# Layer 1's output projection: y's hi and lo in one tile, buffers of their own for the last weights, gate sums as fp32r products

## The chip, the cores and the metric

The kernel runs on one core of a Trainium2 chip. The metric is the device time of one execution in microseconds (us). A profiled execution also has a span, from its first to its last instruction, and all positions below are us from the start of that span.

## The reference

Two trunk layers work on a latent stream x (256 tokens, 2048 wide) and a context stream (256 tokens). Cut to what matters here:

```python
shift, scale, gate = jnp.split(silu_c @ w_mod[l] + b_mod[l], 3, axis=-1)
h = rmsnorm(x, g_pre[l]) * (1.0 + scale[:, None]) + shift[:, None]
proj = h @ w_in[l]
y = mixer_branches(proj, latent_attn, ...)        # 256 x 2048: gMLP, window attention, Fourier parts
y = rmsnorm(y @ w_out[l], g_post[l])
x_new = x + gate[:, None] * y
```

The change is in the last two lines for the last layer: `y @ w_out[1]`, and the gate, which is a row of 2048 numbers made from `silu_c @ w_mod[1]`, `b_mod[1]` and `g_post[1]`.

## The kernel before, in words

**Products in parts.** A number in fp32 is kept as a pair hi + lo of two fp32r tiles: ACT casts it to hi (`A.copy`), DVE subtracts hi from it to get lo. A product of two such pairs is three TensorE products into one sum in PSUM, hi·hi, hi·lo and lo·hi: `mm3`, L405 to L407. In layer 1 the main products of the input projection use `mm2` (L521, L522) instead, on tiles `hh[k]` that hold hi in the columns 0 to 255 and lo in 256 to 511 (for the latents); `hl[k]` holds the same for the context, and is last read by the units k and v.

**Weights.** `Stream` brings all weights in tiles of 128x1024. `load` (L362) issues the DMA of one tile from SP into `raw`, which has three buffers. `emitting` (L367) casts it on ACT into `whi` (L383) and subtracts on DVE into `wlo` (L385); both have four buffers. Tiles named in `self.place` get hi and lo in other buffers: `TAIL` does that for the last four tiles of all (mraw; macc and ws/bsb; yo8 to yo15). `fetch` emits the tiles up to three ahead of the one that is asked for.

**Order.** PE's order is as written. The order of ACT, DVE, SP and POOL is laid out when the program is built, by a planner that goes by its own estimates of times, takes what is ready, and prefers what is written earlier. On the chip each engine then works through its list in that order and stands before an instruction whose operand or buffer isn't there.

**Layer 1's output projection** is `finish` (L961). The 2048 output columns are four chunks c of 512. Each chunk has eight weight tiles, two k (blocks of 128 rows of `w_out`) in each, and two token blocks t: `products` (L983) makes 3 matmuls of 512 columns for one (k, t), with y's parts `hh[k]`, `hl[k]` as the stationary operand. They are made at the end of `layer` (L921 to L925), hi into a fresh `hh[i]`, lo into a fresh `hl[i]`. In the last chunk t=1 runs eight k behind t=0 (`BACK`), so that all its eight tiles stay in use to the end. `evac` (L988) squares the sums on ACT (L990) and multiplies them by the gate on DVE (L992); `close` ends each token block with the norm, the residual and the output DMAs.

**The gate.** `mod_gate1` (L233) forms for each chunk `g1[c]`, a 128x512 tile, in the buffers ctrh, ctrl, nstrh and nstrl: sixteen DVE steps (L242, L244) with weights that SP loads into `mraw` (two buffers). Its column sums, spread over all partitions, come from one product with a tile of ones, in fp32 (L257). `gate1` also loads two rows into ws and bsb (L255) and finishes the gate with two DVE instructions (L258, L259). `GATES` says behind which k of which chunk `gate1(c)` is written. `pace` steps `mod_gate1` along with the weight tiles.

**Later work** is kept in `Later`: generators that say how long they want to wait before their next step; `tick` moves the clock by the time of the products just written. `turn` (L965) runs so in this stage and makes the residual: 32 transposes on PE, eight copies on ACT. `w2k` is a pool of seven tiles for passing work, `join` one of two.

Of the kernel before, what the change touches and what calls it, by code (L numbers as in the profile page):

```python
# [13 lines left out]
P = 128  # L14
# [52 lines left out]
def trunk_kernel(ctx: ExitStack, tc: tile.TileContext, xT, xhalf, cT, wss, wsl, wmod, win, wout0, wout1, const, vec, rows,  # L67
# [9 lines left out]
    def sb(shape, dt, tag, bufs=1):  # L77
        cnt[0] += 1
        return pool.tile(shape, dt, tag=tag, bufs=bufs, name=f"{tag}_{cnt[0]}")
# [8 lines left out]
    def ms_ps(name="ms"):  # L88
        cnt[0] += 1
        return psum.tile([P, 512], F32, tag="ms", bufs=2, name=f"ps_{name}_{cnt[0]}")  # L90
# [160 lines left out]
    def gate1(c):  # L251

        r = [sb([P, 512], F32, tag) for tag in ("ws", "bsb")]
        for i in range(2):
            DMA.dma_start(r[i], rows[None, i, c * 512:(c + 1) * 512].to_broadcast([P, 512]))  # L255
        ps = ms_ps("gate")
        PE.matmul(ps, ones, g1[c], start=True, stop=True)  # L257
        V.tensor_tensor(out=g1[c], in0=r[0], in1=ps, op=ALU.add)  # L258
        V.tensor_tensor(out=g1[c], in0=g1[c], in1=r[1], op=ALU.mult)  # L259

    def mod_rest():
        yield from mod_four(0, range(8, 12))
# [16 lines left out]
    MIDDLE = 3  # L279
    LOWC = 60  # L280
    YT = 3.0
    GATES = {4: 0}, {0: 1}, {0: 2, 14: 3}, {}
    YH = 2.0
    NX, LATE = 4, 6
    YX, YR, YC, YE = 1.0, 0.8, 1.5, 5.0
# [11 lines left out]
    class Later:  # L297
# [19 lines left out]
        def flush(self):  # L317
# [4 lines left out]

    HELD = 3
    NHI, NLO, NRAW = 4, 4, 3
    TAIL = [(("mraw", 2), ("mraw", 2)), (("macc", 1), ("ws bsb", 1)),
            (("yo8 yo9", 1), ("yo10 yo11", 1)), (("yo12 yo13", 1), ("yo14 yo15", 1))]
    AU2 = [(("hh12 hl12", 1), ("hh13 hl13", 1)), (("yo4 yo5", 1), ("yo6 yo7", 1))]
    BACK = 8


    class Stream:
        AHEAD = 3

        def __init__(self):
            self.src, self.out, self.pos, self.stop = [], [], 0, 0
            self.raws = []
            self.place, self.behind = {}, {}
            for l in range(2):
                def half(name, i, h):
                    return win[l, UIDX[name][i], h]  # L340
                for i in range(2):
                    a = [half("av", 2 * i, 0), half("au01", i, 0), half("av", 2 * i, 1),
                         half("av", 2 * i + 1, 0), half("au01", i, 1), half("av", 2 * i + 1, 1)]
                    if l == 0:
                        a.insert(3 - i, half("au2", 0, i))
                        self.place[len(self.src) + 3 - i] = AU2[i]
                    self.src += a
                for i, u in enumerate(UNITS):
                    if u[0] not in ("av", "au01") + ("au2",) * (l == 0):
                        self.src += [win[l, i, 0], win[l, i, 1]]  # L350
                if l == 0:
                    self.src += [wout0[j, i] for j in range(KT) for i in range(2)]
                else:
                    self.src += [wout1[c, i] for c in range(4) for i in range(8)]
                if l == 0:
                    n = len(self.src) - 2 * HELD
                    self.place[n] = (("mraw", 2), ("mraw", 2))
                    self.place[n + 1] = (("macc", 1), ("mg", 1))
            for i, tags in enumerate(TAIL):
                self.place[len(self.src) - len(TAIL) + i] = tags  # L360

        def load(self):  # L362
            r = sb([P, 1024], F32, "raw", NRAW)
            DMA.dma_start(r, self.src[len(self.raws)])
            self.raws.append(r)

        def emitting(self, cut=1024):  # L367

            if len(self.raws) == len(self.out):
                self.load()  # L370
            n = len(self.out)
            r = self.raws[n]
            tags = self.place.get(n, (("whi", NHI), ("wlo", NLO)))
            hi, lo = ([sb([P, 1024 // len(t[0].split())], F32R, tag, t[1]) for tag in t[0].split()] for t in tags)
            self.out.append((hi, lo))
            cut = min(cut, 1024 // max(len(hi), len(lo)))
            for i in range(0, 1024, cut):
                c = slice(i, i + cut)
                ph, pl = part((hi, lo), c)
                with ExitStack() as after:  # L380
                    for i in self.behind.get(n, ()):
                        after.enter_context(tc.issue_after(i.ins))
                    A.copy(ph, r[:, c])  # L383
                yield
                self.last = V.tensor_tensor(out=pl, in0=r[:, c], in1=ph.bitcast(F32), op=ALU.subtract)  # L385
                yield

        def emit(self):
# [164 lines left out]
    def layer(l):  # L553
# [366 lines left out]

        src = [ysl(k) for k in range(KT)]  # L921
        for i, k in enumerate(ORDER):
            new_h(i)
            A.copy(hh[i][:, 0:n], src[k])
            V.tensor_tensor(out=hl[i][:, 0:n], in0=src[k], in1=hh[i][:, 0:n].bitcast(F32), op=ALU.subtract)  # L925


    def o_evac(j, ps, o, acc, streams, first):
# [32 lines left out]
    def finish():  # L961

        x1 = {}

        def turn():  # L965

            for j, tag in enumerate(("vv", "mg", "mgl", "kt0 kt1")):
                tag = tag.split()
                tl = [sb([P, 2 // len(tag), 512], F32, t) for t in tag]
                for t in range(2):  # L970
                    x1[j, t] = tl[0][:, t] if len(tl) == 1 else tl[t][:, 0]
                    ps = ms_ps("x1")
                    for i in range(4):
                        PE.transpose(ps[:, i * P:(i + 1) * P], yo[4 * j + i][:, t * P:(t + 1) * P], ident)
                    A.copy(x1[j, t], ps)
                    yield YT

        later.add(turn(), YT)
        state["phase"] = "out1"
        sums = sb([P, 2, 4], F32, "sums")  # L980
        gy = {}
        tot = sb([P, 2], F32, "tot")
        def products(c, k, t, ps):  # L983
            ts = slice(t * P, (t + 1) * P)
            mm3(ps, (hh[k][:, ts], hl[k][:, ts]), part(w[k // 2], slice((k % 2) * 512, (k % 2 + 1) * 512)),
                k == 0, k == KT - 1)

        def evac(c, t, ps):  # L988
            gy[c, t] = sb([P, 512], F32, f"yo{2 * c + t}")
            A.activation(w2k([P, 512]), ps, AF.Square, accum_out=sums[:, t, c:c + 1])  # L990
            if c < 3:
                V.tensor_tensor(out=gy[c, t], in0=ps, in1=g1[c], op=ALU.mult)  # L992
            if c == 2:
                V.tensor_reduce(out=tot[:, t:t + 1], in_=sums[:, t, 0:3], axis=mybir.AxisListType.X, op=ALU.add)
                V.tensor_scalar(out=tot[:, t:t + 1], in0=tot[:, t:t + 1], scalar1=1.0 / D, scalar2=EPS,  # L995
                                op0=ALU.mult, op1=ALU.add)

        def close(t, ps):
            ms, r = (sb([P, 1], F32, t, 2) for t in ("rs_a", "rs_b"))
            V.tensor_scalar(out=ms, in0=sums[:, t, 3:4], scalar1=1.0 / D, scalar2=tot[:, t:t + 1], op0=ALU.mult,  # L1000
                            op1=ALU.add)
            G.tensor_tensor(out=r, in0=ms, in1=mhalf[:, 0:1], op=ALU.pow)
            V.tensor_tensor(out=gy[3, t], in0=ps, in1=g1[3], op=ALU.mult)
            for c, i, n in ((0, 0, 256), (0, 256, 256), (1, 0, 512), (3, 0, 512), (2, 0, 512)):
                sl = slice(i, i + n)
                o = gy[c, t][:, sl]
                if c == 3:
                    A.activation(o, o, AF.Copy, scale=r)
                    G.tensor_tensor(out=o, in0=o, in1=x1[c, t], op=ALU.add)
                else:  # L1010
                    V.scalar_tensor_tensor(out=o, in0=o, scalar=r, in1=x1[c, t][:, sl], op0=ALU.mult, op1=ALU.add)
                DMA.dma_start(out[t * P:(t + 1) * P, c * 512 + i:c * 512 + i + n], o)

        for c in range(4):
            pss = [mm_ps("y") for _ in range(2)]
            back = BACK if c == 3 else 0
            w = []
            for k in range(KT + back):
                if k < KT:
                    if k % 2 == 0:  # L1020
                        w.append(W.next())
                    products(c, k, 0, pss[0])
                if k == KT - 1:
                    evac(c, 0, pss[0])
                    if c == 3:
                        close(0, pss[0])
                if k >= back:
                    products(c, k - back, 1, pss[1])
                later.tick(PASS * 1024)
                if k in GATES[c]:  # L1030
                    gate1(GATES[c][k])
            evac(c, 1, pss[1])
        close(1, pss[1])

# [225 lines left out]
```

## Time and profile before

| | us |
|---|---|
| median of 3 runs | 1153.36 (1153.26 to 1154.21) |
| profiled execution | 1155.53 |
| its span | 1153.70 |
| PE busy | 1137.0, 99% of the span |
| DVE busy | 883.0, 77% |
| ACT busy | 521.6, 45% |
| first ps_y product (output projection of layer 1) starts | 1046.56 |
| last ps_y product ends | 1145.40 |

In the profile, PE is TensorE's matmuls, DVE VectorE, ACT ScalarE, POOL GpSimd, SP the engine that issues the DMAs. A matmul's length in the profile holds its way through the array, and lengths of successive matmuls overlap, so the cost of one is read from the starts of its neighbours. The granted clock is a share of TensorE's full speed; over the whole span it is 0.997. A group of instructions is named by line, engine, operation, and out<-in by the program's names of tiles without their numbers. A wait for several semaphores is put down to the one that came last by the profile, which need not be the true one. The span is read by stretches, and then one engine at a time in order of time.

### The profile page before, as it was taken

How to read it: one execution, taken by the hardware profiler on the slowest of the kernel's cores; microseconds unless marked ns; L12 is line 12 of the kernel's file. 1: busy time of each engine (PE TensorE's matmuls, PEld its weight loads, DVE VectorE, ACT ScalarE, POOL GpSimd, SP SyncE). 2: the span in 40 equal slices, each digit the busy share in tenths (PEclk: the TensorE clock that was granted, in tenths of full speed). 3: DMA queues.
4: the chain of work that ended last, by engine and by line, in shares of the span. 5: the costliest groups of instructions: out<-in, count | busy, mean ns of one | idle time of the engine just before them, and what ended most of it. 6: DMA issues, size and time to landing. Idle time of an engine off the chain costs nothing.

```text
span 1153.7 us, 17000 instructions
## 1 busy us (share of the span) xinstructions
PE 1137.0 (99%) x6391; PEld 935.2 (81%) x6391; DVE 883.0 (77%) x1496; ACT 521.6 (45%) x956; POOL 32.4 (3%) x39
## 2 busy tenths in 40 slices
PE   8999999999999999999999999999999999999996
PEld 3566688888898888888888888888888988888875
DVE  1545479999988887888999993396988688868774
ACT  5322343322224667632532323366665279846441
POOL 0000000000000000000000000200500000000001
PEclk9999999999999999999999999999999999999998
DMA  9999756566665343355566654365956666556972
GB/s 353 403 369 340 253 183 182 168 220 213 202 185 198 108 124 126 116 188 180 164 203 217 218 183 146 110 193 182 219 164 202 204 215 195 171 164 221 297 233 107
DMA packets 72227, 234.30 MB, mean 203 GB/s; under 512 B 8400, under 2 KB 11600, under 8 KB 72144
## 3 DMA queue, kind: packets, MB, share of 16 engines
q1 hardware_dynamic: 69840, 231.11, 61.4%
q0 software_dynamic: 2304, 2.10, 1.2%
q8 instruction: 50, 0.82, 0.3%
q14 instruction: 33, 0.27, 0.1%
HBM read 231.08 MB, written 2.10 MB: 202 GB/s over the span
## 4 chain that ended last, share of the span: by engine, by line
PE 85%; DMA 8%; DVE 4%; issue 2%; ACT 1%; SPq 0%; POOL 0%; DVEq 0%; ACTq 0%; POOLq 0%
PE ps_t L405 15%; PE ps_t L407 15%; PE ps_t L406 15%; PE ps_t L521 10%; PE ps_t L522 5%; DMA mraw<-in_wmod_dram 3%; PE ps_mod L169 2%; PE ps_av L405 2%; PE ps_av L406 2%; PE ps_av L407 2%; PE ps_tp L849 2%; DVE wlo L385 1%; PE ps_v L406 1%; PE ps_v L407 1%; PE ps_v L405 1%
## 5 line engine op out<-in xcount | busy, mean ns | idle before, releaser
L383 ACT CAST whi<-raw 128x1024 fp32r<-128x1024 f32 (+1 forms) x218 | 226.6, 1043 | 342.4 <-PE ps_t L406 222.7
L385 DVE TENSOR_TENSOR wlo<-raw,whi 128x1024 fp32r<-128x1024 f32 (+1 forms) x218 | 263.6, 1213 | 74.9 <-ACT whi L383 73.1
L405 PE MATMUL ps_t<-hh,whi 128*128 128x512 f32 (+1 forms) x768 | 294.2, 383 | 1.0 <-ACT yo L709 1.0
L407 PE MATMUL ps_t<-hh,wlo 128*128 128x512 f32 (+1 forms) x768 | 292.6, 381 | 0.0
L406 PE MATMUL ps_t<-hl,whi 128*128 128x512 f32 (+1 forms) x768 | 292.5, 381 | 0.0
L206 DVE SCALAR_TENSOR_TENSOR macc<-mraw,cs,macc 128x512 f32<-128x512 f32 x360 | 249.6, 748 | 17.8 <-DMA mraw<-in_wmod_dram 17.7
L521 PE MATMUL ps_t<-hh,whi 128*128 128x512 f32 x512 | 185.2, 400 | 0.0
L405 PEld LDWEIGHTS ps_t<-hh,whi 128*128 128x128 f32 x768 | 144.4, 188 | 29.1 <-issue 1.5
L407 PEld LDWEIGHTS ps_t<-hh,wlo 128*128 128x128 f32 x768 | 144.4, 188 | 27.9
L406 PEld LDWEIGHTS ps_t<-hl,whi 128*128 128x128 f32 x768 | 144.5, 188 | 26.0 <-issue 0.2
L522 PE MATMUL ps_t<-hh,wlo 128*128 128x256 f32 x512 | 143.1, 280 | 0.0
L521 PEld LDWEIGHTS ps_t<-hh,whi 128*128 128x128 f32 x512 | 96.2, 188 | 21.2 <-issue 0.2
L522 PEld LDWEIGHTS ps_t<-hh,wlo 128*128 128x128 f32 x512 | 96.5, 189 | 0.2 <-issue 0.2
L487 ACT ACTIVATE hh<-w2k,sh 128x256 fp32r<-128x256 f32 x48 | 21.9, 503 | 82.3 <-DVE w2k L483 82.3
L405 PE MATMUL ps_y<-whi,hh 128*128 128x512 f32 x112 | 46.4, 415 | 0.6 <-ACT whi L383 0.6
L406 PE MATMUL ps_y<-wlo,hh 128*128 128x512 f32 x112 | 44.2, 394 | 1.2 <-DVE tot L995 1.2
L407 PE MATMUL ps_y<-whi,hl 128*128 128x512 f32 x112 | 44.2, 395 | 0.0
L405 PE MATMUL ps_av<-whi,hh 128*128 128x512 f32 x96 | 39.7, 413 | 0.6 <-ACT hh L487 0.6
L406 PE MATMUL ps_av<-wlo,hh 128*128 128x512 f32 x96 | 38.0, 396 | 0.4 <-DVE wlo L385 0.4
L422 ACT CAST w2k<-ps_tp 128x512 fp32r<-128x512 f32 x40 | 23.4, 585 | 23.1 <-PE ps_scc L406 12.7
L435 POOL TENSOR_TENSOR rs_b<-rs_a,mhalf 128x2 f32<-128x2 f32 (+1 forms) x7 | 7.5, 1066 | 797.1 <-DVE rs_a L433 797.1
L829 ACT ACTIVATE w2k<-w2k,den 128x512 f32<-128x512 f32 (+1 forms) x48 | 27.9, 645 | 1.8 <-DVE den L825 1.6
(365 smaller groups left out, 1746.7 us busy)
## 6 DMA issues: line engine op xcount, KB each, us to landing
raw<-in_win_dram SPq DMA_DIRECT2D x160, 512.0 KB, 3.7
mraw<-in_wmod_dram SPq DMA_DIRECT2D x128, 512.0 KB, 4.3
raw<-in_wout_dram SPq DMA_DIRECT2D x64, 512.0 KB, 4.5
mraw<-in_wsl_dram SPq DMA_DIRECT2D x16, 512.0 KB, 6.6
yo<-in_xT_dram SPq DMA_DIRECT2D x16, 256.0 KB, 5.4
macc<-in_wsl_dram SPq DMA_DIRECT2D x8, 512.0 KB, 7.6
vv<-in_wsl_dram SPq DMA_DIRECT2D x8, 512.0 KB, 8.3
mg<-in_wsl_dram SPq DMA_DIRECT2D x8, 512.0 KB, 5.5
```

What stands on the lines that cost most here:

```text
L169: PE.matmul(ps[32 * kk:32 * kk + 32, 0:n], cpad[:, kg * 4 + kk], ws[kk], start=kg == 0, stop=kg == 3, tile_position=(0, 32 * kk))
L206: V.scalar_tensor_tensor(out=acc[:, s], in0=w[:, kk % 2], scalar=c, in1=acc[:, s], op0=ALU.mult, op1=ALU.add)
L383: A.copy(ph, r[:, c])
L385: self.last = V.tensor_tensor(out=pl, in0=r[:, c], in1=ph.bitcast(F32), op=ALU.subtract)
L405: PE.matmul(ps, st[0], mv[0], start=start, stop=False)
L406: PE.matmul(ps, st[0], mv[1], start=False, stop=False)
L407: PE.matmul(ps, st[1], mv[0], start=False, stop=stop)
L422: A.copy(hi, src)
L521: PE.matmul(ps, w[0], h, start=k == 0, stop=False)
L522: PE.matmul(ps[:, 0:S], w[1], h[:, 0:S], start=False, stop=k == KT - 1)
L829: A.activation(prob[i][:, b * w:(b + 1) * w], prob[i][:, b * w:(b + 1) * w], AF.Copy, scale=den[:, c:c + 1])
L849: PE.transpose(tp[:, (2 * j + b) * P:(2 * j + b + 1) * P], src, ident)
```

## The change

It has four parts.

1. y's lo goes into the second half of the `hh[i]` tile whose first half holds hi; the sixteen `hl` tiles take no part in the output projection any more, and `products` reads its stationary operands by `h_of(1, k, ts)`.
2. Those tiles become buffers: hl0 to hl7 for hi and lo of two more weight tiles in `TAIL` (now six), hl8 to hl15 for the raw data of the last four, each loaded as two DMAs of 512 columns. A tile that lies in halves is cast and subtracted in halves.
3. `gate1` becomes a generator: it loads the rows and splits `g1[c]` into hi and lo (two w2k tiles), waits `YG`, sums both parts with fp32r products against a copy of the ones in fp32r (in a join buffer), and ends as before.
4. `GATES` moves: gate 0 from chunk 0, k=4 to k=2; gate 1 from chunk 1, k=0 to chunk 0, k=14; gate 2 from chunk 2, k=0 to chunk 1, k=14; gate 3 from chunk 2, k=14 to k=12. The first step is taken at the next tick, the product three ticks later (each 1.296 us by the kernel's own clock): behind k=6 of chunk 0, k=2 of chunk 1, k=2 of chunk 2 and k=0 of chunk 3.

```diff
+        parts = split_into(w2k([P, 512], F32R), w2k([P, 512], F32R), g1[c])
+        yield YG
         ps = ms_ps("gate")
-        PE.matmul(ps, ones, g1[c], start=True, stop=True)
+        for i, t in enumerate(parts):
+            PE.matmul(ps, state["ones"], t, start=i == 0, stop=i == 1)
         V.tensor_tensor(out=g1[c], in0=r[0], in1=ps, op=ALU.add)
         V.tensor_tensor(out=g1[c], in0=g1[c], in1=r[1], op=ALU.mult)
+        yield 0.0
...
-    GATES = {4: 0}, {0: 1}, {0: 2, 14: 3}, {}
+    GATES = {2: 0, 14: 1}, {14: 2}, {12: 3}, {}
+    YG = 3.0
...
-    TAIL = [(("mraw", 2), ("mraw", 2)), (("macc", 1), ("ws bsb", 1)),
+    TAIL = [(("hl0 hl1", 1), ("hl2 hl3", 1)), (("hl4 hl5", 1), ("hl6 hl7", 1)),
+            (("mraw", 2), ("mraw", 2)), (("macc", 1), ("ws bsb", 1)),
             (("yo8 yo9", 1), ("yo10 yo11", 1)), (("yo12 yo13", 1), ("yo14 yo15", 1))]
+    TAILRAW = ["hl8 hl9", "hl10 hl11", "hl12 hl13", "hl14 hl15"]
...
+            self.raw_place = {len(self.src) - len(TAILRAW) + i: tags for i, tags in enumerate(TAILRAW)}
...
         def load(self):
-            r = sb([P, 1024], F32, "raw", NRAW)
-            DMA.dma_start(r, self.src[len(self.raws)])
+            n = len(self.raws)
+            if n in self.raw_place:
+                r = [sb([P, 512], F32, tag) for tag in self.raw_place[n].split()]
+                for i, t in enumerate(r):
+                    DMA.dma_start(t, self.src[n][:, i * 512:(i + 1) * 512])
+            else:
+                r = sb([P, 1024], F32, "raw", NRAW)
+                DMA.dma_start(r, self.src[n])
             self.raws.append(r)
...
-            cut = min(cut, 1024 // max(len(hi), len(lo)))
+            cut = min(cut, 1024 // max(len(hi), len(lo), len(r) if isinstance(r, list) else 1))
...
-            new_h(i)
-            A.copy(hh[i][:, 0:n], src[k])
-            V.tensor_tensor(out=hl[i][:, 0:n], in0=src[k], in1=hh[i][:, 0:n].bitcast(F32), op=ALU.subtract)
+            if last:
+                hh[i] = sb([P, T], F32R, f"hh{i}")
+                split_into(hh[i][:, 0:S], hh[i][:, S:T], src[k])
+            else:
+                new_h(i)
+                split_into(hh[i], hl[i], src[k])
...
+        state["ones"] = sb([P, P], F32R, "join", 2)
+        A.copy(state["ones"], ones)
...
-            mm3(ps, (hh[k][:, ts], hl[k][:, ts]), part(w[k // 2], slice((k % 2) * 512, (k % 2 + 1) * 512)),
+            mm3(ps, h_of(1, k, ts), part(w[k // 2], slice((k % 2) * 512, (k % 2 + 1) * 512)),
                 k == 0, k == KT - 1)
...
                 if k in GATES[c]:
-                    gate1(GATES[c][k])
+                    later.add(gate1(GATES[c][k]))
```

More of the change, by code (lines that the diff above doesn't have):

```diff
@@ L379, in emitting @@
                 ph, pl = part((hi, lo), c)
+                rc, _ = part((r, r), c)
                 with ExitStack() as after:
@@ L382, in emitting @@
                         after.enter_context(tc.issue_after(i.ins))
-                    A.copy(ph, r[:, c])
+                    A.copy(ph, rc)
                 yield
-                self.last = V.tensor_tensor(out=pl, in0=r[:, c], in1=ph.bitcast(F32), op=ALU.subtract)
+                self.last = V.tensor_tensor(out=pl, in0=rc, in1=ph.bitcast(F32), op=ALU.subtract)
                 yield
```

## The prediction

> **What bounds the kernel now.** I first read the busy time by stretch, with edges laid at layer 1's output projection (columns: us, then busy us and count of each engine, granted TensorE clock, DMA share, GB/s).
>
> ```profile
> 1046.50:1071.00 24.50, 24.50 (x118) 20.00 (x117) 21.28 (x34) 13.56 (x22) 0.00 (x0) 1.00 0.74 238
> 1071.00:1095.50 24.50, 24.50 (x114) 19.94 (x113) 17.89 (x23) 10.19 (x15) 0.00 (x0) 1.00 0.90 297
> 1095.50:1119.00 23.50, 23.50 (x102) 18.74 (x101) 17.47 (x20) 10.62 (x13) 0.00 (x0) 1.00 0.79 255
> ...
> 1123.20:1125.70 2.50, 0.70 (x3) 0.20 (x2) 2.50 (x8) 1.80 (x3) 0.00 (x0) 1.00 0.57 162
> 1125.70:1129.20 3.50, 3.50 (x9) 2.73 (x10) 2.50 (x5) 1.14 (x2) 0.00 (x0) 0.51 0.53 186
> 1129.20:1145.40 16.20, 16.18 (x70) 12.78 (x68) 5.41 (x8) 2.56 (x5) 1.84 (x2) 1.00 0.13 46
> ```
>
> PE is full throughout but for one hole of 2.5 us in the last quarter, and the 3.5 us behind the hole run at a clock of 0.51. So time can be won in two ways: by fewer PE cycles, or by closing that hole. The PE rows in order of time show the hole and a gate sum (start, length, then idle before and its releaser in brackets):
>
> ```profile
> 1116.66 0.39 PE L407 MATMUL ps_y<-whi,hl 128*128 128x512 f32 x1
> 1116.89 1.02 PE L257 MATMUL ps_gate<-nstrl,ones 128*128 128x512 f32 x2
> 1117.34 0.79 PE L405 MATMUL ps_y<-whi,hh 128*128 128x512 f32 x1
> 1117.97 0.39 PE L406 MATMUL ps_y<-wlo,hh 128*128 128x512 f32 x1
> ...
> 1123.00 0.39 PE L407 MATMUL ps_y<-whi,hl 128*128 128x512 f32 x1
> 1124.01 0.50 PE L405 MATMUL ps_y<-whi,hh 128*128 128x512 f32 x1 [0.62 <-ACT whi L383]
> 1125.69 0.72 PE L406 MATMUL ps_y<-wlo,hh 128*128 128x512 f32 x1 [1.18 <-DVE tot L995]
> 1126.21 0.63 PE L407 MATMUL ps_y<-whi,hl 128*128 128x512 f32 x1
> ```
>
> Lengths overlap, so cost is read from starts: products of 512 columns follow each other at 0.227 us. The 1.18 us put down to `tot` is really L385 writing wlo just ahead of it. ACT's order says why that weight tile was late:
>
> ```profile
> 1116.47 1.05 ACT L383 CAST whi<-raw 128x1024 fp32r<-128x1024 f32 x1 [1.42 <-DMA raw<-in_wout_dram]
> 1120.81 1.05 ACT L383 CAST mraw<-raw 128x1024 fp32r<-128x1024 f32 x1 [3.29 <-DMA raw<-in_wout_dram]
> 1121.77 0.59 ACT L990 ACTIVATE w2k<-ps_y 128x512 f32<-128x512 f32 x1
> 1122.92 1.04 ACT L383 CAST whi<-raw 128x1024 fp32r<-128x1024 f32 x1
> ```
>
> I number the stage's 32 weight tiles 0 to 31, eight to each of the four column chunks. Tile 27 may enter a whi buffer only when tile 23 is consumed (1119.1). The planner put tile 28 (into mraw) ahead of it, and tile 28's raw load, issued at 1116.34, landed at 1120.79. ACT stood 3.29 us behind that load, then did two L990 squares, and only then tile 27.
>
> **The change part by part.** All times are of the profiled execution: 1155.53 us, span 1153.70. The median shown is 1153.36, 2.17 lower; I take the difference from the one and subtract it from the other.
>
> *The hole.* From 1123.00 to 1129.45 PE starts 11 products: 6.45 us where 11 x 0.227 = 2.50 would do. The loss is **3.95 us**: 0.78 for hi, 1.45 for lo, 1.72 of slow clock (eight steps of 0.43). With buffers of their own for the parts of tiles 26 and 27 (hl0 to hl7) and for raw 28 to 31 (hl8 to hl15), tile 27 waits neither for tile 23 nor behind raw 28. What is late next? Raw 27 was issued at 1114.57; 4.5 us to landing (median of these loads) gives 1119.1, a half cast of 0.62 (yo<-raw, 128x512) 1119.7, a half subtraction of 0.69 1120.4. PE comes for it at about 1121.6 (below). ACT's two squares (0.79 each) and DVE's two L992 (0.68 each) can eat that margin of 1.2 but not much more. I take all 3.95; the other end is nothing.
>
> *Early raw loads.* Eight loads of 256 KB replace four of 512 KB. hl8 to hl15 are last read by v, whose products end at 924.5, and the planner issues a load as soon as its buffer is free: L255's ws load is written behind k=4 of the projection (1053.9) and was issued at 962.3. So 2 MB move to about 925, at a cost of 8 x 0.33 us on SP. Queued behind them are raw tiles for q and mraw. From 840 to 1040 DMA is 0.61 busy and no PE wait is listed; 2 MB at the 350 GB/s that the busiest slices reach is 6 us, against four whi buffers that each last 2.9 us (q) to 5.5 us (v). I take nothing; the bound is one raw tile late, some 2 us, and no gain either way, PE being full there.
>
> *Gate sums.* L257 in fp32: from 1116.66 to 1117.97 is 1.31 us where two steps would be 0.45, so 0.855 each, and the same at the other three. Two fp32r products of the same width as ps_y's cost 2 x 0.227 = 0.455. That saves 0.40, four times: **1.6 us**. If fp32r moving data cost what fp32 does here, the saving would be nothing or a loss of 0.855 each; all of ps_y is fp32r at 0.227, so I take 0.40. Each sum now also needs an ACT copy (0.59, as w2k<-ps_tp) and a DVE subtraction (0.69), and `ones` a copy of 128 columns (under 0.4). PE would queue behind a late part, and all ps_y products with it. The parts are asked for three ticks (3.9 us) ahead of the product, more than 0.59 + 0.69 and one L385 of 1.22 in front; gate 0 meets DVE at its fullest (1045 to 1055, no idle), where two L385 in front would make PE wait about 0.5. I take nothing here, and keep 0.5 as a bound.
>
> *hi and lo of y in one tile.* The same 16 casts (0.41) and 16 subtractions (0.42); the last ends at 1051.8 where its product comes at 1067. If products had to wait for both halves, product k=0 would wait for the subtraction at 1043.6, and it starts at 1046.6. Nothing.
>
> *Crowding.* Into chunks 1 and 2 the change moves the subtractions of tiles 28, 30 and 31 (1.4 each) and two gate parts: 5.5 us on top of 23.98 of 32 DVE us from 1087 to 1119, so 92% full. The tightest tile is 20: its lo was ready at 1106.4, wanted at 1107.6, and after three cheaper gates is wanted at 1106.4. I charge **0.3**, half of one more 0.69 in front. For tile 27: chunk 3 now starts at 1119.1 - 1.2 - 0.855 (gate 3 moves behind its first k) = 1117.05; six k of 0.68 and a gate of 0.455 give 1121.6.
>
> Sum: 3.95 + 1.6 - 0.3 = **5.25 us less**: span 1148.4, median **1148.1**. The tail behind the last product (8.3 us) does not change.
>
> [...] The row first: two waits of 0.78 and 1.45, with 0.70 us of work in 2.5, then 3.5 us at 0.51. [...]
>
> **The rivals.**
> 1. *The weights come late elsewhere* (16%). For: the margin at tile 20 and DVE at 92%; SP reloads raw only behind L385, so each late subtraction delays a load too. Against: once the last mraw work ends (1107.06) three tiles cycle in some 6 us (subtractions 20, 23, 26 end at 1106.4, 1112.9, 1118.8) where PE uses 8.2. A wait of 1 to 2 us, with the clock's 1.72 if they gather in 2.5 us: 1149.4 to 1152, near 1151.
> 2. *It doesn't do what it says* (5%): the early loads stay queued near 1116, tile 27 is as late as before, only the gates gain: 1151.8. Against: L255 at 962.
> 3. *The clock falls anyway* (4%): 1148.1 + 1.72 = 1149.8. [...] Against: the granted clock is 1.00 in every other stretch from 800 on, though PE waited 0.87 at 825.
> 4. *Slower: ACT again behind a late operand* (11%). Gate 3's hi copy waits for nstrl, finished at 1107.06 after mraw loads of 5.5 to 6.5 us. Placed ahead of tile 21's cast: copy to 1107.65, cast to 1108.7, lo to 1109.9, wanted at 1109.1: 0.8 us lost. One landing later (6.5) it is 7.3 + 1.72 = 9.0, against 5.55 won: **1156.9**. It turns slower once nstrl ends after 1110.1 (0.8 + 3.0 + 1.72 = 5.5). For: just this order of ACT made the present hole. Against: nstrl's loads keep their place.
>
> **How the numbers follow.** The forecast has 64%, by itself 1147.0 (no charge, and some of the 0.7 us of smaller irregular steps in this stage gone) to 1149.4. Faster by over 0.2% (2.3 us, about what a measurement can tell from no change) means below 1151.05: forecast 64, clock 4, ten of rival 1: 78%. Within 0.2%: six of rival 1 and rival 2: 11%. Slower: rival 4: 11%. The range 1147.0 to 1152.0 takes in rivals 1 to 3 and the bounds of 0.5 and 2 us, and leaves out rival 4 and little below.
>
> **What would show it.** Right: L257 as two fp32r rows and 0.455 per sum; hl8 to hl15 loaded from in_wout near 925; no PE wait above 0.3 us and a clock of 1.00 from 1046 to the last product, which ends near 1140. Wrong: a listed PE wait on wlo or on a gate part, a slow-clock stretch with no wait before it, or PE waits from 920 to 960. The forecast fails if tile 27 still comes after 1121.6, or if tiles 17 to 22 slip by over 1 us.

## The result and the profile after

| | before | after |
|---|---|---|
| median, taken in turn on one chip | 1154.21 (1153.26 to 1155.07, 9 runs) | 1151.36 (1149.75 to 1155.19, 9 runs) |
| ratio | | 0.998 [0.997, 0.9989] |
| profiled execution | 1155.53 | 1150.26 |
| its span | 1153.70 | 1148.5 |
| first to last weight load of ps_y | 98.31 | 93.57 |

The medians lie 2.85 us apart, and the interval of the ratio, 1.3 to 3.5 us, is clear of no change. The forecast was a median of 1148.1, 5.25 us less; the measured one is 3.3 us above it, though inside the range. Of these 3.3 us, 2.4 are a gain that came out smaller, and 0.85 come from the kernel before, whose median here is 1154.21 where the forecast started from 1153.36. The span of the profiled execution, forecast as 1148.4, came out at 1148.5. How both can be so is the point of this document.

The stage in stretches (us, then busy us and count of PE, weight loads, DVE, ACT, POOL; granted clock, DMA share, GB/s). The hole and the slow stretch, which were at 1123.2 to 1129.2, are gone:

```profile
1095.50:1119.00 23.50, 22.95 (x102) 18.66 (x101) 19.37 (x24) 10.93 (x15) 0.00 (x0) 1.00 0.73 243
1119.00:1121.50 2.50, 2.50 (x13) 2.07 (x12) 2.13 (x5) 2.02 (x6) 0.00 (x0) 1.00 0.01 3
1121.50:1125.70 4.20, 4.20 (x20) 3.45 (x19) 3.07 (x8) 0.00 (x0) 0.00 (x0) 1.00 0.02 4
1125.70:1129.20 3.50, 3.50 (x17) 2.85 (x16) 0.00 (x0) 0.00 (x0) 0.00 (x0) 1.00 0.00 0
```

PE is full there at a clock of 1.00. The first line lacks 0.55 us of PE, which was not so before. The PE rows show where it went, with a good gate sum for comparison:

```profile
1056.29 0.62 PE L260 MATMUL ps_gate<-w2k,join 128*128 128x512 f32 x2
1056.75 0.40 PE L420 MATMUL ps_y<-whi,hh 128*128 128x512 f32 x1
...
1098.17 0.39 PE L260 MATMUL ps_gate<-w2k,join 128*128 128x512 f32 x1
1099.11 0.50 PE L260 MATMUL ps_gate<-w2k,join 128*128 128x512 f32 x1 [0.55 <-DVE w2k L438]
1099.44 0.39 PE L420 MATMUL ps_y<-whi,hh 128*128 128x512 f32 x1
```

Gate 0 takes 1056.75 - 1056.29 = 0.46 us, as forecast. Gate 2 takes 1.27: its lo part was subtracted only at 1098.37 to 1099.05, and PE stood before the second product. Its hi part and DVE's list show why:

```profile
1094.19 0.61 ACT L437 CAST w2k<-nstrh 128x512 fp32r<-128x512 f32 x1
...
1095.18 1.54 DVE L244 SCALAR_TENSOR_TENSOR nstrl<-mraw,cs,nstrl 128x512 f32<-128x512 f32 x2 [1.56 <-DMA mraw<-in_wmod_dram]
1096.63 1.22 DVE L400 TENSOR_TENSOR wlo<-raw,whi 128x1024 fp32r<-128x1024 f32 x1
...
1098.37 0.68 DVE L438 TENSOR_TENSOR w2k<-nstrh,w2k 128x512 fp32r<-128x512 f32 x1
```

The hi part was there at 1094.80. DVE had two steps of gate 3 (L244) ahead of the subtraction in its list and stood 1.56 us for their load; those steps, the subtraction of a weight tile (1.22) and a multiplication by the gate (0.68) then had to pass first. It is the pattern of the hole once more, on DVE. ACT's list at the end of the stage shows the new order:

```profile
1113.86 1.05 ACT L398 CAST whi<-raw 128x1024 fp32r<-128x1024 f32 x1 [0.96 <-DMA raw<-in_wout_dram]
1116.27 1.14 ACT L398 CAST hl<-raw 128x512 fp32r<-128x512 f32 x2 [1.36 <-DMA raw<-in_wout_dram]
1118.71 1.14 ACT L398 CAST hl<-raw 128x512 fp32r<-128x512 f32 x2 [1.29 <-DMA raw<-in_wout_dram]
1119.76 0.59 ACT L1010 ACTIVATE w2k<-ps_y 128x512 f32<-128x512 f32 x1
```

The casts into hl are tiles 26 and 27. Tile 28 was cast at 1102.14 already. Nothing stands between tile 27 and its data but its own load, and the squares come behind it. SP issued the eight early raw loads between 913.94 and 924.02, close to where the prediction put them; four of them stand in one line:

```profile
916.44 3.58 SPq L375 DMA_DIRECT2D hl<-in_wout_dram  x4
```

```profile
840.00:1040.00 200.00, 200.00 (x1250) 179.08 (x1250) 159.89 (x281) 128.52 (x246) 0.00 (x0) 1.00 0.64 200
```

PE is busy for 200.00 of these 200 us, with DMA at 0.64.

### The profile page after: what moved, and what is told of

Read it like the earlier page. It is cut to its first block, busy times and chain, and to the rows that moved or that the text cites. A ratio compares the mean times of both kernels' runs of the same rounds, so it can differ in the third digit from the quotient of the medians.

```text
span 1148.5 us, 17015 instructions
## 1 busy us (share of the span) xinstructions
PE 1132.7 (99%) x6387; PEld 934.0 (81%) x6391; DVE 884.7 (77%) x1503; ACT 523.0 (46%) x964; POOL 32.4 (3%) x39
## 4 chain that ended last, share of the span: by engine, by line
PE 87%; DMA 5%; DVE 4%; issue 2%; ACT 1%; SPq 0%; POOL 0%; DVEq 0%; ACTq 0%; POOLq 0%
PE ps_t L420 15%; PE ps_t L422 15%; PE ps_t L421 15%; PE ps_t L536 10%; PE ps_t L537 5%; PE ps_mod L169 2%; PE ps_av L420 2%; PE ps_av L421 2%; PE ps_av L422 2%; DMA mraw<-in_wmod_dram 2%; DVE wlo L400 2%; PE ps_tp L864 2%; PE ps_v L421 1%; PE ps_v L422 1%; PE ps_v L420 1%
## 5 line engine op out<-in xcount | busy, mean ns | idle before, releaser
L398 ACT CAST whi<-raw 128x1024 fp32r<-128x1024 f32 (+1 forms) x216 | 224.3, 1041 | 333.2 <-PE ps_t L421 224.6
L400 DVE TENSOR_TENSOR wlo<-raw,whi 128x1024 fp32r<-128x1024 f32 (+1 forms) x216 | 260.8, 1210 | 71.9 <-ACT whi L398 69.8
L420 PE MATMUL ps_y<-whi,hh 128*128 128x512 f32 x104 | 41.3, 397 | 0.0
L422 PE MATMUL ps_y<-whi,hh 128*128 128x512 f32 x104 | 40.6, 390 | 0.0
L421 PE MATMUL ps_y<-wlo,hh 128*128 128x512 f32 x104 | 40.5, 390 | 0.0
```

Of the source, the lines that this page charges most:

```text
L398: A.copy(ph, rc)
L400: self.last = V.tensor_tensor(out=pl, in0=rc, in1=ph.bitcast(F32), op=ALU.subtract)
L420: PE.matmul(ps, st[0], mv[0], start=start, stop=False)
L421: PE.matmul(ps, st[0], mv[1], start=False, stop=False)
L422: PE.matmul(ps, st[1], mv[0], start=False, stop=stop)
```

## The experiments

In the texts on record, "the stage" is layer 1's output projection, its length is taken from the first to the last weight load of ps_y, and tiles are numbered as in the prediction.

**After, once more.** The kernel after, unchanged.

> The changed kernel once more, to see how its executions scatter. The nine shown so far run from 1149.75 to 1155.19 us with a median of 1151.36, where the kernel before runs from 1153.26 to 1155.07; the profiled one has a span of 1148.5, as forecast (1148.4). Theory W (weights just in time): in other executions some weight tile of chunks 1 or 2 comes late, PE waits and the clock falls behind the wait. Theory G (gate): the gate's lo part, for which PE waits 0.8 us in the profiled execution, comes later still in others. Theory E (early loads): the loads into hl8 to hl15 near 920 disturb units q. All three expect the same here: 1150 to 1155 us, median near 1151.5, ratio near 0.998.

Measured: 1151.04 (1150.43 to 1152.15, 11 runs), ratio 0.9972 [0.996, 0.9985]; span 1149.3, stage 93.30, gate 2's sum 0.99. The wide scatter of the first nine runs did not come back: eleven runs lie within 1.7 us. So the theories made for it have nothing to work on here; what made two of the first nine long (1153.72 and 1155.19) stays open. The first gain is confirmed: 2.6 us between these medians, and the interval, 1.7 to 4.6 us, leaves out 5.25.

**The gate sums alone**, in the kernel before (the edits of `gate1`, `GATES` and `YG`, its call by `later.add` and the ones in fp32r, as in the diff of the change; nothing else):

> The kernel before with the gate part alone: fp32r products of hi and lo, the new places, the ones in a join buffer; y's tiles, TAIL and raw as before. Without the buffers the hole in front of tile 27 should stay (3.95 us), so at best 1.6 us less than before. Theory G: the gate's waits alone make executions scatter by 3 us or more, and the median is within 1 us of before. Theory W: the stream has the same early draw from cheaper gates, so it scatters too, but with waits on L385's lo and not on gate parts. Theory E: 1.6 us less and a scatter of under 2 us, as before.

Measured: 1151.0 (1150.38 to 1151.94, 8 runs), ratio 0.9976 [0.9966, 0.9986]; span 1148.6, stage 93.00, gate 2's sum 0.68, and no PE wait for tile 27. The gate sums alone give as much as the whole change. This was not foreseen: with the gates' new instructions and places the planner laid out ACT's list anew, and in it tile 27's cast (into whi) stands ahead of tile 28's (into mraw):

```profile
1118.29 1.04 ACT L388 CAST whi<-raw 128x1024 fp32r<-128x1024 f32 x1
1119.58 1.05 ACT L388 CAST mraw<-raw 128x1024 fp32r<-128x1024 f32 x1 [0.26 <-DMA raw<-in_wout_dram]
```

The hole went as a by-product.

**The buffers alone** (after, with the gate sums of before at their old places):

> The changed kernel with its gate in fp32 at the old places, called at once: only the buffers and y's shared tile. Theory G: the hole is gone and nothing scatters: 1154.2 - 3.95 = 1150.2, within 2 us from lowest to highest. Theory W: a lowest near 1150.2, but a scatter of 3 us or more, as the subtractions of tiles 28, 30 and 31 still crowd DVE in chunks 1 and 2. Theory E: the same as W, with waits near 920 to 960.

Measured: 1151.78 (1151.35 to 1152.72, 11 runs), ratio 0.9981 [0.9972, 0.999]; span 1150.3, stage 94.37, no PE wait and a clock of 1.00 throughout the stage. Against the 1153.62 of before in the same series (25 runs) the buffers are worth 1.84 us. The prediction had 3.95 for just this. The gate sums, added to the buffers, give 0.74 more (1151.04 in the same series).

**Without the early raw loads.**

```diff
-    TAILRAW = ["hl8 hl9", "hl10 hl11", "hl12 hl13", "hl14 hl15"]
+    TAILRAW = []
```

> The changed kernel without buffers of their own for the last four raw tiles (TAILRAW empty), so they take their turn in raw and land after 1114 again; all else as changed. Theory E: the scatter shrinks to under 2 us and the median falls to 1149. Theory W: with tiles 28, 30 and 31 subtracted late again, DVE is less crowded in chunks 1 and 2, so less scatter there, but the end of the stream is late again in part: 1150 to 1153. Theory G: as the changed kernel, 1151.4 with the same scatter.

Measured: 1150.91 (1149.97 to 1151.93, 6 runs), ratio 0.9972 [0.9961, 0.9984]; span 1148.9, stage 93.22. The same as after (1151.04): loading the last four raw tiles near 920 costs nothing and gains nothing that can be measured. Whether the buffers for tiles 26 and 27 matter beside the new gate sums, this run can't show, since the gate sums alone reach the same time.

**Before, three more profiles.** If the buffers give 1.84 and the hole was 3.95, one of the two is not typical. So three more executions of the kernel before were profiled:

> The kernel before, for the trace of another execution. Its profiled execution took 1155.53 us, 2.2 above the median of its runs, with 3.95 us lost between 1123.0 and 1129.5. Theory S (size): that execution was not typical; where a time near 1153.4 is measured, the hole in front of tile 27 loses only some 1.8 us, which is what the buffers alone won (1153.62 to 1151.78), mostly without the slow clock. Theory U (upstream): the hole loses 3.9 us in every execution, the 2.2 us lie ahead of the output projection, and the buffers gave 2 us back elsewhere.

> The kernel before once more, for the same question: theory S expects that the loss between tile 26 and tile 28 differs from execution to execution (0 to 4 us) and goes with the time; theory U expects 3.9 us again.

> The kernel before a third time, as the two above: S 0 to 4 us, going with the time; U 3.9 us.

Measured: spans 1151.6, 1151.0 and 1153.4; stages 96.05, 95.86 and 98.29. In the first, PE's rows in the hole:

```profile
1123.42 0.50 PE L405 MATMUL ps_y<-whi,hh 128*128 128x512 f32 x1
1125.10 0.50 PE L406 MATMUL ps_y<-wlo,hh 128*128 128x512 f32 x1 [1.17 <-DVE tot L995]
1125.43 0.39 PE L407 MATMUL ps_y<-whi,hl 128*128 128x512 f32 x1
1125.66 0.40 PE L405 MATMUL ps_y<-whi,hh 128*128 128x512 f32 x1
```

The wait for lo is there in full (1125.10 - 1123.42 - 0.23 = 1.45), the one for hi, whose product comes 0.33 behind the one at 1123.09, has shrunk to 0.10, and the products behind follow at 0.23 us: no slow clock (the granted clock reads 1.00 in every stretch from 1118 to 1133). The hole is 1.7 us in this execution. In the second there is no wait for hi, and the one for lo is shorter (1124.51 - 1122.95 - 0.23 = 1.33); the hole is 1.45:

```profile
1122.95 0.40 PE L405 MATMUL ps_y<-whi,hh 128*128 128x512 f32 x1
1124.51 0.50 PE L406 MATMUL ps_y<-wlo,hh 128*128 128x512 f32 x1 [1.16 <-DVE tot L995]
```

The third is like the execution that the prediction was made from, 0.76 for hi and 1.45 for lo, then slow clock (0.50 in the stretches from 1126 to 1128), 3.9 in all:

```profile
1122.70 0.39 PE L407 MATMUL ps_y<-whi,hl 128*128 128x512 f32 x1
1123.69 0.50 PE L405 MATMUL ps_y<-whi,hh 128*128 128x512 f32 x1 [0.60 <-ACT whi L383]
1125.37 0.69 PE L406 MATMUL ps_y<-wlo,hh 128*128 128x512 f32 x1 [1.18 <-DVE tot L995]
```

The first product of the stage starts at 1046.56 in the execution that the prediction was made from, and at 1046.65, 1046.25 and 1046.26 in these three. That differs by less, and not in step with the spans, so the surplus of the long executions is made inside the stage. The expectation that the hole differs between executions, and not what lies upstream of it, held.

**The order on ACT alone.** In the kernel before, one edge of order: tile 28's cast is issued behind tile 27's. No buffer, load or product differs.

```diff
+                    if n == len(self.src) - len(TAIL):
+                        after.enter_context(tc.issue_after(self.cast.ins))
-                    A.copy(ph, r[:, c])
+                    self.cast = A.copy(ph, r[:, c])
```

> The kernel before with one edge for the planner: tile 28's cast is issued behind tile 27's on ACT; no buffer, no gate is changed. Theory O (order): the hole is ACT standing behind raw 28, so it closes by the order alone: cast 27 follows the two squares near 1120.7, its lo is ready near 1123.5, PE loses at most 0.5 us, the clock stays at 1.00, and the median is that of the buffers alone, 1151.8 (1151.3 to 1152.5). Theory B (buffers): tile 27 still waits for tile 23's whi buffer and then for its turn on DVE, so PE still loses 1 to 2 us and the median is 1153 or more.

Measured: 1151.74 (1150.93 to 1152.48, 12 runs), ratio 0.9974 [0.9962, 0.9985]; span 1149.5, stage 94.40, no PE wait. ACT's rows:

```profile
1118.39 0.60 ACT L992 ACTIVATE w2k<-ps_y 128x512 f32<-128x512 f32 x1 [1.86 <-PE ps_y L409]
...
1119.66 1.04 ACT L385 CAST whi<-raw 128x1024 fp32r<-128x1024 f32 x1
1120.60 1.05 ACT L385 CAST mraw<-raw 128x1024 fp32r<-128x1024 f32 x1
```

Tile 27 is cast at 1119.66 where it was 1122.92, with the same three raw buffers and tile 28's load issued at 1115.56, near before's 1116.34. Both medians, this one and that of the buffers, are 1151.7 to 1151.8. Over the whole kernel the lists of ACT and DVE differ from before's in three places: tile 28's cast and, with it, its subtraction on DVE went behind tile 27's, and one small step of the norm (0.15) went ahead of tile 27's subtraction. So the hole was the order, as the prediction read it, and one edge buys all that the new buffers buy here.

**Gate 2 written earlier**, in after and in the kernel with the gate sums alone:

```diff
-    GATES = {2: 0, 14: 1}, {14: 2}, {12: 3}, {}
+    GATES = {2: 0, 14: 1}, {9: 2}, {12: 3}, {}
```

> The changed kernel with gate 2 written behind k=9 of chunk 1 in place of k=14, so its parts are split some 6.8 us earlier and its product comes behind k=13 of chunk 1. Theory G2: in every trace of the new gates the sum of gate 2 takes 0.67 to 1.27 us where the others take 0.46, since its lo part waits on DVE; moved early it takes 0.46, so 0.2 to 0.8 us are won: median 1150.5 where the changed kernel has 1151.0, no PE wait in the stage. Rival: the lo part is late wherever it stands, since DVE is full; then the wait moves along and the median stays at 1151.0.

> The gate part alone, with gate 2 early as in the run above; no buffers. If the hole in front of tile 27 is only a matter of the order on ACT (in the gate part alone tile 27 is cast ahead of tile 28), this is as fast as the run above, 1150.5, within 0.5 us. If the buffers give something of their own, it is slower by 0.5 or more.

Measured, with all buffers: 1150.88 (1150.27 to 1151.96, 7 runs), ratio 0.9975 [0.9963, 0.9986]; span 1148.5, stage 92.86, the lowest of all. The wait is gone:

```profile
1092.08 0.63 PE L260 MATMUL ps_gate<-w2k,join 128*128 128x512 f32 x2
1092.54 0.39 PE L420 MATMUL ps_y<-whi,hh 128*128 128x512 f32 x1
```

Gate 2 takes 0.46 and no PE wait is listed from 1045 to 1140. In the stage that is 0.44 less than in after's second profile; the medians (1151.04 and 1150.88, of different series) don't tell it apart. The rival, that the lo part is late wherever it stands, is out.

Without the buffers the second of the two outcomes set out came, slower by more than 0.5: 1153.66 (1151.58 to 1154.02, 11 runs), ratio 0.9989 [0.9979, 0.9999], stage 96.67. The move was meant to take a small wait away, and larger ones came:

```profile
1113.01 0.50 PE L411 MATMUL ps_y<-wlo,hh 128*128 128x512 f32 x1 [0.55 <-DVE wlo L390]
1122.25 0.50 PE L411 MATMUL ps_y<-wlo,hh 128*128 128x512 f32 x1 [0.27 <-DVE wlo L390]
1125.43 0.50 PE L411 MATMUL ps_y<-wlo,hh 128*128 128x512 f32 x1 [1.51 <-DVE wlo L390]
```

PE stands behind lo parts of weight tiles, tile 27's among them (1125.43). Tile 27's cast stands ahead of tile 28's here too (1122.00 and 1123.30 on ACT), so the good order of these two casts is not enough by itself. The move let the planner lay out everything behind it anew, and that layout has no room. So the buffers are worth 2.8 us here (1153.66 and 1150.88 in one series) and nothing in the layout of the gate sums alone (1151.0 and 1151.04): of the two orders tried, they save the unlucky one.

**A longer wait for tile 27.** The kernel with the one edge, and eight more copies of 512 columns on ACT ahead of tile 27's cast (work added; nobody reads the copies):

```diff
+                    if n == len(self.src) - len(TAIL) - 1:
+                        for _ in range(8):
+                            d = A.copy(w2k([P, 512]), r[:, 0:512])
+                            after.enter_context(tc.issue_after(d.ins))
```

> The kernel before with tile 28 behind tile 27, and eight extra ACT copies of 128x512 (about 0.5 us each, results unused) just ahead of tile 27's cast, so that tile 27 is late by design: hi ready near 1124.7 where PE wants it at 1123.0, lo some 1.3 later, so PE waits about 3.0 us in two pieces. Theory C (clock with the wait): waits of 2.2 us or more in this place bring 3.5 us at half clock, so 1.7 more is lost: 4.7 in all, median 1151.7 + 4.7 = 1156.4, the clock near 0.5 for 3.5 us in the trace. Rival: the slow clock of two of the four traces of before comes by itself; then 1154.7 and a clock of 1.00 in some executions.

Measured: 1156.38 (1155.58 to 1157.78, 10 runs), ratio 1.0025 [1.0016, 1.0034]; span 1154.4, stage 97.47. The median is the one expected with the slow clock, but in the profile there was none: waits of 1.93 and 1.03 us (from the starts, less the 0.23 of a product), and a granted clock of 1.00 to the last product. Chunk 0 had started at 1048.00, later than in any other profile, and so the sum matched by accident. One more profile was to tell which part comes back:

> The delayed order_fix once more (eight more copies on ScalarE ahead of tile 27's cast, nothing left out), one look, to see which parts of its first execution come back. If the delay upstream belongs to the kernel, chunk 0 starts near 1048.1 again and the span is near 1154.4; if it was the usual scatter of about 1 us, it starts near 1046.7 and the span is near 1153.0. If a wait of over 3 us brings the slow clock only by chance, the stage may show 0.5 to 0.7 granted clock behind tile 27 this time (some 1.7 us more, span near 1154.7); if this wait never does, it shows 1.00 again with a hole near 3.2.

Measured: 1156.73, span 1155.0. Chunk 0 started at 1046.99, and the slow clock came. The two profiles side by side, the one without it first:

```profile
1126.60 0.50 PE L411 MATMUL ps_y<-whi,hh 128*128 128x512 f32 x1 [1.77 <-ACT whi L389]
1127.86 0.50 PE L412 MATMUL ps_y<-wlo,hh 128*128 128x512 f32 x1 [0.76 <-DVE wlo L391]
```

```profile
1125.62 0.50 PE L411 MATMUL ps_y<-whi,hh 128*128 128x512 f32 x1 [1.77 <-ACT whi L389]
1126.88 0.50 PE L412 MATMUL ps_y<-wlo,hh 128*128 128x512 f32 x1 [0.76 <-DVE wlo L391]
```

The waits agree to 0.01 us, and the first kept its clock while the second lost half of it for 3.4 us (lines in the last section); its stage is 99.05 long, 1.58 more. So the length of the wait alone does not decide (what the profiles show of it stands in the last section), and the late start of chunk 0 was scatter upstream. That all ten timed runs lie within 2.2 us fits such sums, but the runs without a profile can't be split.

## Why the prediction was wrong

**The step that failed** is how the sum was carried to the median: "The median shown is 1153.36, 2.17 lower; I take the difference from the one and subtract it from the other." The one is the profiled execution (1155.53, span 1153.70). The first term of that difference, the hole at **3.95**, was the hole of that one execution. It held 0.78 for hi and 1.72 of slow clock, and other executions of the same kernel hold 0.10 or nothing of the first and nothing of the second: the hole is 1.7 and 1.45 in two of four profiles, 3.9 in the other two. The two edits that close the hole and leave the gates alone took 1.84 (buffers) and 2.13 (one edge, 1153.87 to 1151.74) off the median. So the term was too large by about 2, and the surplus of the profiled execution over the median, 2.17, fits the difference between a long hole and a short one (98.31 and 98.29 for the stage against 96.05 and 95.86). The surplus was noted as a number, and the whole hole was then counted as gain below a median that, by what these edits took off it, did not contain all of it.

That the profiled execution of after took 1150.26, where 1155.53 - 5.25 is 1150.28, is largely luck. Its stage is 4.74 us shorter, 3.94 for the hole (by the buffers alone) and 0.80 for the gates, where the sum had 3.95 and 1.6 - 0.3. The rest is an upstream start 0.74 earlier, which the forecast didn't have, less a tail 0.28 longer; and this execution lies 1.1 us below the median of its nine.

**The hole's cause was right.** ACT stood 3.29 us behind raw 28; with one edge of order, and nothing else in the source, PE's wait is gone. The closing of the hole by the buffers was right as well, and so was the margin: tile 27's parts came in time. The slow clock came only behind the wait: none of the seven profiles without the hole (after, a1 to a4, c1, d1) shows it inside the stage, and in after, a1, c1 and d1 the granted clock reads 1.00 in every stretch from 1118 to 1133.

**Gate sums**: 0.455 forecast, 0.46 measured for gates 0, 1 and 3. Between the profiles of the buffers alone and of the kernel with gate 2 written earlier the stage loses 1.51 us, against 1.6. In after itself it loses 0.80 and 1.07 (two profiles), and 0.74 between the medians, less than the 1.3 that is left of 1.6 after the charge of 0.3.

**Crowding**: 0.3 was charged to weight tiles late in chunk 2, and none of those were late. The loss was at gate 2's lo part, 0.2 to 0.8 us in the four profiles that have it. The prediction had bounded a late gate part by 0.5, and had looked for it at gate 0, where DVE is fullest. It came at gate 2, and not because DVE was full: in all four profiles DVE stood 1.56 to 1.89 us for a load of mraw, with the lo part behind the steps of that load in its list. With the gate written earlier the wait is gone.

**Early raw loads**: near 920 and free, as forecast; worth nothing either.

**The rivals.** Weights late elsewhere, no effect, and ACT behind nstrl: none of them shows in after's trace (gate 3's hi copy ran at 1107.54, and PE did not wait for it). The price of the fourth comes to 1156.8 by its own terms, not 1156.9. The clock did not fall in after's stage; its largest wait there is 0.81 us.

**A better sum**, in hindsight, was to be had from more profiles of before: 1.6 for a short hole, 1.6 for the gates, less 0.3, is 2.9, and so 1150.5; measured were 2.6 and 2.9 us between medians taken in turn. That it comes so near is partly luck too, as the buffers gave 1.84 and the gates then 0.74.

## What to carry to other kernels

Ahead of subtracting a stall from a median, compare the profiled execution with the median: if it is the longer by about as much as part of the stall, profile the kernel again and size the stall by what every profile shows. When an engine stands behind a late operand with a ready instruction queued behind, try one edge of order before buffers; but keep the buffers if the order is laid out by a planner that a small edit can upset. And an edit whose instructions pass through such a planner is to be judged by the new order of the engines, since the gate sums alone closed a hole that they do not touch.

## What was not expected of the hardware

Inside the stage, a slow stretch had the same length each time. In the three profiles that have one there, the granted clock was at 0.50 for 3.41 to 3.42 us: from 1125.80 to 1129.21 in before as profiled, from 1125.51 to 1128.93 in its third further profile, from 1127.59 to 1131.00 in the second profile of the delayed kernel. The stretches of 3.41 us ahead of the fall and behind it read as follows. Before as profiled:

```profile
1122.39:1125.80 3.41, 1.61 (x7) 0.79 (x6) 3.41 (x9) 2.61 (x6) 0.00 (x0) 1.00 0.47 138
1125.80:1129.21 3.41, 3.41 (x9) 2.64 (x10) 2.40 (x4) 1.14 (x2) 0.00 (x0) 0.50 0.51 179
```

The delayed kernel's second profile, with the slow clock:

```profile
1120.77:1124.18 3.41, 3.08 (x14) 2.23 (x12) 0.82 (x4) 3.41 (x8) 0.00 (x0) 1.00 0.28 114
1124.18:1127.59 3.41, 1.21 (x4) 0.81 (x5) 1.99 (x2) 3.38 (x5) 0.00 (x0) 1.00 0.00 0
1127.59:1131.00 3.41, 3.41 (x10) 2.62 (x9) 1.58 (x4) 0.66 (x2) 0.00 (x0) 0.50 0.77 262
```

Its first profile, without it inside the stage, and the half clock that it shows only behind the last product:

```profile
1123.00:1126.41 3.41, 1.82 (x9) 1.17 (x7) 0.20 (x2) 3.41 (x6) 0.00 (x0) 1.00 0.11 43
1126.41:1129.83 3.42, 2.48 (x10) 1.81 (x11) 3.25 (x4) 2.12 (x4) 0.00 (x0) 1.00 0.25 48
...
1150.31:1153.72 3.41, 0.00 (x0) 0.00 (x0) 0.71 (x2) 0.00 (x0) 0.00 (x0) 0.50 0.62 231
```

So PE was not idle ahead of a fall: the 3.41 us before it held 1.61, 1.63 (the third further profile of before) and 1.21 us of work. Nor does little work alone bring a fall: 1124.70 to 1128.20 of the delayed kernel's first profile holds only 0.97 in 3.50 us, and the clock stayed. In the other profiles with waits that kept the clock, the stretches of 3.50 us read around the wait hold no less than 1.74 us (gate 2 early without the buffers), 2.33 and 2.34 (the first two further profiles of before). Where the waits are equal, the slow stretch cost 1.58 us of stage (99.05 against 97.47).

Why the same waits bring the half clock in one execution and not in another, no run shows. The author's estimate goes by positions: in before as profiled the clock falls at 1125.80 and again, behind the last product, at 1149.70, and these 23.90 us are seven times 3.414. If the changes lay at whole steps of that length in the delayed kernel too, then, counted back from 1150.31 in its first profile, an edge would stand at 1126.41 and cut the waits into steps with 1.82 and 2.48 us of work, while in its second profile they fall almost whole into the one step with 1.21. What looks like chance at a given wait would then be where the steps lie in that execution. No experiment moved them, and the line between fall and stay is not drawn exactly: a step so laid at the end of before's first further profile (1141.69 to 1145.11) held 1.53, and the clock stayed through the next.
